# Where the last pair's scores stand against the first block inverse, and how the inversion's steps are dealt out

## The chip, the cores and the metric

One core of one Trainium2 chip runs the whole kernel as one program. The metric is device time in microseconds of that core, and the figure for a kernel is the median of its runs. Before the change it is 1244.08 us, the median of three runs from 1243.03 to 1244.97.

## The reference, cut to what matters

Four residual sub-layers over 512 positions of 1024 channels: a gated spatial mixer, a gated convolutional feed-forward layer, an RWKV-7 time mixer, and the feed-forward layer again, each behind an RMS norm. The change lies in the time mixer. With 16 heads of 64 channels it computes

```
...
r = xr @ w_r;  k = xk @ w_k;  v = xv @ w_v
...
def step(state, inp):                       # state (head, 64 values, 64 keys)
    sa = state @ a_t
    state = state * w_t + sa b_t^T + v_t k_t^T
    y_t = state @ r_t
...
y = group_norm(y) * ln_w + ln_b
bonus = sum(r * k * r_k) * v
return ((y + bonus) * (sigmoid(xg @ g1) @ g2)) @ w_o
```

Everything is in float32.

## The kernel before, in words

**Dense products.** A dense 128x512 product is made of three TensorE matmuls of high and low parts (lines 325, 326, 327). A group of 24 of them makes one block of 128 output channels. In the time mixer these groups are the *fill*: a generator that yields after every six matmuls (two blocks of 128 inputs), so that other work on TensorE can be put between the steps. `fill` is a chain of three generators: `projections` (keys and values), `gates` (the gate's first factor, lines 1135 and 1172 among others) and `project` (the output projection, `wo`). `gates` and `project` also yield when they have nothing to give: `gates` calls `idle` (line 1124: two matmuls whose result nobody uses) until the first group of heads has been normalised, and `project` yields nothing at all while the group's gated outputs are not yet emitted.

**The chunked scan.** The recurrence is done in 8 chunks of 64 positions, with heads in 8 pairs; pairs 0 to 3 are group 0, pairs 4 to 7 group 1. The stages, in the order of the program:

1. `pairs` makes, for each pair, decayed operands (lines 911 to 957, mostly VectorE), then the *scores* inside a chunk and the *turned keys* (`products`: matmuls at lines 973 and 988; VectorE's masked copies at line 977). A pair is three yields.
2. `invert(g)` inverts the triangular 64x64 matrices of group g: 25 yields. The first is taken before anything is woven. Then come 15 yields of substitution, on VectorE alone: lines 1069 and 1070, a product and an addition into the same tile, so that each waits for the one before it. Two transposes follow (line 1051), then eight yields of small TensorE products, 16 matmuls of 32x32 at a time (lines 1090 and 1093): the *block inverse's products*. ScalarE writes their results back into `ti[g]`.
3. `scan(g)`: for each chunk four small TensorE batches (lines 1301 and 1305, 1314, 1321, 1326) with copies by VectorE and ScalarE between them (1304, 1315 and 1316, 1325). The batch at line 1314 needs `ti[g]`. Behind every second chunk `finish` normalises the output (lines 1342 to 1366; the reciprocal root on GpSimd, line 389), and `gate` multiplies it with the gate (lines 1201 to 1214).

**What sets the order.** `weave(main, side, fill, rate, lag, side_rate)` runs `main`; after each of its yields it adds `rate` to a debt of fill steps and `side_rate` to a debt of side steps, and pays whole ones. `RATES` holds these numbers, one tuple for each of five weaves. Before the change the second weave (pairs 4 to 6 and the first yield of pair 7, with `invert(0)` at the side) and the weave for the last two yields of pair 7 both pay 2.2 steps of the inversion per yield of `pairs`. A layer below orders the recorded instructions on each engine's queue; each queue then runs strictly in that order.

**The values' bonus.** Inside a fill group of values, `value` puts two more matmuls between its steps: line 868, and line 883, whose result VectorE multiplies at line 885. Both, and the dense group itself, take a PSUM bank under the name `mm`, of which there are two. One is held by the dense group that is running, so the next dense group opens in the bank that line 885 has read.

Of the kernel before, what the change touches and what calls it, by code (L numbers as in the profile page):

```python
# [29 lines left out]
GN_EPS = 64e-5  # L30
C1 = -0.5 * math.exp(-0.5)

RATES = ((1.9, 2), (1.9, 6, 2.2), (0.66, 2, 1.15), (0.72, 2), (1.2, 6, 2.2))
LEAD = 1
WB = 4
FIRST0, WAIT, STEPS = 1, 1, (2, 2, 2, 2)
# [108 lines left out]
class Emit:  # L145
# [622 lines left out]
    def rwkv_main(self, r, ctx, gain):  # L768
# [226 lines left out]
        def pairs():  # L995

            units = [type("Unit", (), {})() for _ in range(KT)]

            def start(p):
                if p >= KT:  # L1000
                    return iter(())
                while p not in ks:
                    next(fill)
                if p == 0:
                    second_factors(p)
                return decay(p, units[p])

            yield from start(0)
            nxt = start(1)
            operands(0, units[0])  # L1010
            for _ in nxt:
                yield
            for p in range(KT):
                nxt = start(p + 2)
                if p + 1 < KT:
                    operands(p + 1, units[p + 1])
                parts = products(p, units[p])
                for n in range(3):
                    next(nxt, None)
                    with ExitStack() as behind:  # L1020
                        if n < 2:
                            behind.enter_context(tc.issue_after(self.last(mybir.EngineType.PE)))
                        next(parts, None)
                    yield
                done.add(p)

        def invert(g):

            tg = ti[g].rearrange("p i c t -> p (i c) t")
            Q = [(slice(64 * hd + 32 * b, 64 * hd + 32 * b + 32), slice(32 * b, 32 * b + 32))
                 for hd in range(2) for b in range(2)]

            def blocks(tag):
                return ip.tile([P, 32, 32], F32, tag=tag, bufs=1 if tag == "off" else 2, name=self.uid(tag))

            x = blocks("ix")
            pr = ip.tile([P, 272], F32, tag="pr", bufs=1, name=self.uid("pr"))
            cut = 24 * g  # L1040
            for us in (slice(0, cut), slice(cut, 32))[1 - g:]:
                for rows, cols in Q:
                    if us.start and g == 1:
                        V.tensor_copy(x[rows, us], tg[rows, us, cols])
                    else:
                        S.copy(x[rows, us], tg[rows, us, cols])
                if g == 1 and us.start == 0:
                    yield
            def turn(out, src):
                for bs in [slice(n, n + 8) for n in range(0, 32, 8)] if g == 1 else [slice(0, 32)]:  # L1050
                    V.transpose(out[:, bs], src[:, bs])

            tt = blocks("li")
            turn(tt.rearrange("p s t -> p t s"), x.rearrange("p u t -> p t u"))
            V.memset(tt.rearrange("p s t -> p (s t)")[:, 0:1024:33], 1.0)
            for _ in range(WAIT):
                yield
            for j in range(1, 31):
                ni = 31 - j
                to = tt[:, 0:j, j + 1:32]  # L1060
                if j == 1:
                    V.scalar_tensor_tensor(to[:, 0], tt[:, 1, 2:32], tt[:, 0, 1:2], to[:, 0], ALU.mult, ALU.add)
                elif ni == 1:
                    V.scalar_tensor_tensor(to[:, :, 0], tt[:, 0:j, j], tt[:, j, 31:32], to[:, :, 0], ALU.mult, ALU.add)
                else:
                    a = tt[:, j, j + 1:32].unsqueeze(1).to_broadcast([P, j, ni])
                    b = tt[:, 0:j, j].unsqueeze(2).to_broadcast([P, j, ni])
                    q = pr[:, 0:ni * j].rearrange("p (c i) -> p c i", i=ni)
                    V.tensor_tensor(q, a, b, ALU.mult)
                    V.tensor_tensor(to, to, q, ALU.add)  # L1070
                if j % 2 == 1:
                    yield

            z, y = blocks("ix"), blocks("li")
            turn(z.rearrange("p u t -> p t u"), tt)
            if g == 0:
                next(fill)
            turn(y.rearrange("p u t -> p t u"), tt.rearrange("p s t -> p t s"))
            yield
            off, own = blocks("off"), iter(Q)  # L1080
            for i in range(2):
                for hf in range(2):
                    ps = self.acc("aux" if g == 1 else "e").rearrange("p (u t) -> p u t", t=32)
                    us = slice(16 * hf, 16 * hf + 16)
                    for u in range(16):
                        for hd in range(2):
                            b0, b1 = Q[2 * hd][0], Q[2 * hd + 1][0]
                            n = 16 * hf + u
                            if i == 0:
                                nc.tensor.matmul(ps[b1, u, :], tg[b0, n, 32:64], z[b0, n, :], start=True, stop=True,  # L1090
                                                 tile_position=(b0.start, b1.start))
                            else:
                                nc.tensor.matmul(ps[b0, u, :], off[b1, n, :], y[b1, n, :], start=True, stop=True,
                                                 tile_position=(b1.start, b0.start))
                        if u % 8 == 7:
                            if i == 0:
                                rows, cols = next(own)
                                S.copy(tg[rows, :, cols], y[rows])
                            yield
                    for hd in range(2):  # L1100
                        b0, b1 = Q[2 * hd][0], Q[2 * hd + 1][0]
                        if i == 0:
                            S.copy(off[b1, us], ps[b1])
                        else:
                            S.copy(tg[b0, us, 32:64], ps[b0])

        gx, tail = [], []

        def gate_mix(k):
            with ExitStack() as behind:  # L1110
# [272 lines left out]
        def project():  # L1383

            for g in range(2):
                while g not in gated:
                    yield
                for m in range(2 - 2 * g, KT):
                    if m % 2 == 0:
                        w = wo.take()  # L1390
                    a = self.acc("mm")
                    yield from self.dense_steps(a, w, outs[g], c0=m % 2 * 512)
                    with ExitStack() as behind:
                        if left is None:
                            behind.enter_context(tc.issue_after(self.last(mybir.EngineType.DVE)))
                        V.tensor_tensor(self.h[m], self.h[m], a, ALU.add)
                    if g == 1:
                        self.absorb(m, gain)
# [13 lines left out]
        def until(gen, end):  # L1412
            for _ in gen:
                yield
                if end():
                    return


        fill = itertools.chain(projections(), gates(), project())
        gw, ga = {}, {}  # L1420
        main = pairs()
        self.weave(until(main, lambda: 3 in done), None, fill, *RATES[0], ktiles=STEPS[0])
        inv = invert(0)
        for _ in take(inv, FIRST0):
            pass
        self.weave(until(main, lambda: KT - 2 in done), inv, fill, *RATES[1], ktiles=STEPS[1])
        load(0, 0)
        ahead = invert(1)
        next(ahead)
        self.weave(main, inv, fill, *RATES[4], ktiles=STEPS[1])  # L1430
        for _ in inv:
            next(fill)
            self.step(ahead, (mybir.EngineType.PE,))
        ctx.close()
        ep = ctx.enter_context(tc.tile_pool(name="scan", bufs=1))
        inv = ahead
        r.sg = [ep.tile([P, T], F32R, name=f"sg{i}") for i in range(3)]
        for _ in range(LEAD):
            next(fill, None)
        self.weave(scan(0), inv, fill, *RATES[2], ktiles=STEPS[2])  # L1440
        for _ in inv:
            pass
        self.weave(scan(1, left.pop()), None, fill, *RATES[3], ktiles=STEPS[3])
        rest, left = left.pop(), None
# [80 lines left out]
```

## Time and profile before

| what | value |
|---|---|
| median of three runs | 1244.08 us |
| profiled execution, device time | 1245.55 us |
| profiled execution, span from first to last instruction | 1243.7 us |
| TensorE (PE) busy | 1226.8 us, 99% of the span |
| VectorE (DVE) busy | 851.1 us, 68% |
| ScalarE (ACT) busy | 633.1 us, 51% |
| GpSimd (POOL) busy | 81.4 us, 7% |
| mean granted TensorE clock | 0.996 |
| `pairs` 4 to 7 with the first inversion at the side | about 651 to 716 us of the span |
| first scan starts | 725.8 us |
| last dense step before the output projection of group 1 | ends about 848 us |

The profiled execution is one run of its own; the sums of the prediction are made on its scale. A TensorE row of the timeline gives a start and a modelled duration: dense 128x512 matmuls follow each other every 0.23 us although each is shown with 0.39, so the cost of one is read from start to start. The number in square brackets at the end of a row is the engine's idle time just ahead of it, with the instruction that released it.

### The profile page before, as it was taken

What the parts mean: (1) busy time and instruction counts of PE and PEld (TensorE: products, weight loads), DVE (VectorE), ACT (ScalarE), POOL (GpSimd) and SP (SyncE); (2) the same over time, 40 slices, a digit from 0 to 9 for tenths busy, and PEclk for the clock granted to TensorE, in tenths of its full rate; (3) what the DMA queues carried; (4) which work ended last, traced back from release to release, by engine and by line L of the source; (5) the groups of instructions that cost most, each with busy time, mean ns of one, the idle gap of its engine ahead of it and who ended that gap; (6) DMA issues with size and microseconds to landing.
All of it is one profiled execution on the core that took longest, in us unless ns stands there. A gap on an engine that the chain in (4) does not pass through costs nothing.

```text
span 1243.7 us, 19411 instructions
## 1 busy us (share of the span) xinstructions
PE 1226.8 (99%) x7535; PEld 1000.2 (80%) x7535; DVE 851.1 (68%) x1418; ACT 633.1 (51%) x1089; POOL 81.4 (7%) x106
## 2 busy tenths in 40 slices
PE   9999999999999999999999999999999999999997
PEld 6878888888888888877887777778888888888886
DVE  5566578888876454675899698776777777872323
ACT  6544455555554343466787667424544444543232
POOL 1100200000000001000000013222000000000000
PEclk9999999999999999999999899999999999999999
DMA  7232457887556776326888797654223223333332
GB/s 273 94 105 82 132 180 246 246 249 241 192 172 193 220 226 196 109 81 182 220 242 237 188 280 233 219 171 135 85 102 102 90 97 102 97 88 104 97 93 81
DMA packets 125133, 201.65 MB, mean 162 GB/s; under 512 B 39857, under 2 KB 63153, under 8 KB 125041
## 3 DMA queue, kind: packets, MB, share of 16 engines
q10 hardware_dynamic: 38976, 112.87, 29.5%
q1 hardware_dynamic: 86064, 87.54, 22.6%
q8 instruction: 59, 0.97, 0.3%
q14 instruction: 34, 0.27, 0.1%
HBM read 152.93 MB, written 47.45 MB: 161 GB/s over the span
## 4 chain that ended last, share of the span: by engine, by line
PE 91%; DVE 4%; DMA 3%; ACT 1%; issue 0%; SPq 0%; POOL 0%; DVEq 0%; POOLq 0%; ACTq 0%
PE mm L325 9%; PE mm L327 9%; PE mm L326 9%; PE aux L325 6%; PE aux L326 6%; PE aux L327 6%; PE e L325 6%; PE e L326 6%; PE us L325 6%; PE e L327 6%; PE us L327 6%; PE us L326 6%; PE us L1314 1%; PE aux L973 1%; PE aux L988 1%; PE us L1321 1%
## 5 line engine op out<-in xcount | busy, mean ns | idle before, releaser
L237 ACT CAST w<-w 128x512 fp32r<-128x512 f32 x340 | 206.5, 611 | 359.8 <-PE aux L327 92.6
L238 DVE TENSOR_TENSOR w<-w,w 128x512 fp32r<-128x512 f32 x340 | 230.5, 680 | 180.2 <-ACT w L237 179.6
L325 PE MATMUL mm<-mxh,w 128*128 128x512 f32 x408 | 167.9, 412 | 2.7 <-DVE rt L885 2.6
L327 PE MATMUL mm<-mxh,w 128*128 128x512 f32 x408 | 161.1, 395 | 0.0
L326 PE MATMUL mm<-mxl,w 128*128 128x512 f32 x408 | 160.6, 394 | 0.0
L325 PEld LDWEIGHTS mm<-mxh,w 128*128 128x128 f32 x408 | 77.0, 189 | 22.8 <-DVE rt L885 3.3
L327 PEld LDWEIGHTS mm<-mxh,w 128*128 128x128 f32 x408 | 77.0, 189 | 17.1 <-issue 0.8
L326 PEld LDWEIGHTS mm<-mxl,w 128*128 128x128 f32 x408 | 77.1, 189 | 16.2 <-issue 1.7
L575 ACT ACTIVATE cv<-z,par 128x512 f32<-128x512 f32 x88 | 71.7, 817 | 26.5 <-DVE z L573 21.2
L325 PE MATMUL aux<-mxh,w 128*128 128x512 f32 x216 | 84.5, 391 | 0.0
L325 PE MATMUL us<-mxh,w 128*128 128x512 f32 x216 | 84.5, 391 | 0.0
L327 PE MATMUL aux<-mxh,w 128*128 128x512 f32 x216 | 84.2, 390 | 0.0
L326 PE MATMUL aux<-mxl,w 128*128 128x512 f32 x216 | 84.1, 389 | 0.0
L326 PE MATMUL us<-mxl,w 128*128 128x512 f32 x216 | 84.1, 389 | 0.0
L327 PE MATMUL us<-mxh,w 128*128 128x512 f32 x216 | 84.1, 389 | 0.0
L354 POOL TENSOR_TENSOR ss<-ss,sq 128x512 f32<-128x512 f32 x24 | 31.7, 1323 | 761.1 <-ACT sq L352 761.1
L325 PE MATMUL e<-mxh,w 128*128 128x512 f32 x208 | 81.4, 391 | 0.0
L326 PE MATMUL e<-mxl,w 128*128 128x512 f32 x208 | 81.1, 390 | 0.0
L327 PE MATMUL e<-mxh,w 128*128 128x512 f32 x208 | 81.0, 389 | 0.0
L576 DVE SCALAR_TENSOR_TENSOR cv<-z,par,cv 128x512 f32<-128x512 f32 x88 | 66.0, 752 | 19.5 <-ACT cv L575 19.5
L577 DVE SCALAR_TENSOR_TENSOR cv<-z,par,cv 128x512 f32<-128x512 f32 x88 | 66.0, 752 | 2.9
L325 PEld LDWEIGHTS aux<-mxh,w 128*128 128x128 f32 x216 | 40.5, 188 | 9.0 <-issue 0.5
(1113 smaller groups left out, 2555.2 us busy)
## 6 DMA issues: line engine op xcount, KB each, us to landing
w<-in_wup ACTq DMA_DIRECT2D x88, 512.0 KB, 3.7
w<-in_wdn ACTq DMA_DIRECT2D x32, 512.0 KB, 3.7
st<-std SPq DMA_DIRECT2D x15, 640.0 KB, 6.6
w<-wkd ACTq DMA_DIRECT2D x16, 512.0 KB, 5.1
w<-wvd ACTq DMA_DIRECT2D x16, 512.0 KB, 5.1
w<-wod ACTq DMA_DIRECT2D x16, 512.0 KB, 4.2
w<-in_wdn ACTq DMA_DIRECT2D x16, 384.0 KB, 3.3
w<-in_wsu ACTq DMA_DIRECT2D x8, 512.0 KB, 3.7
```

The costliest lines, as they stand in the source:

```text
L237: nc.scalar.copy(hi[r, :n], src)
L238: (lo_eng or nc.vector).tensor_tensor(lo[r, :n], src, hi[r, :n].bitcast(F32), ALU.subtract)
L325: mm(acc, wh, xh, start=first, stop=False)
L326: mm(acc, wh, xl, start=False, stop=False)
L327: mm(acc, wl, xh, start=False, stop=last)
L354: nc.gpsimd.tensor_tensor(self.ss, self.ss, self.sq, ALU.add)
L575: nc.scalar.activation(c, z[:, 2:], AF.Identity, scale=cw(2, i), bias=self.p("conv_b", l * 44 + i))
L576: nc.vector.scalar_tensor_tensor(c, z[:, 1:T + 1], cw(1, i), c, ALU.mult, ALU.add)
L577: nc.vector.scalar_tensor_tensor(c, z[:, 0:T], cw(0, i), c, ALU.mult, ALU.add)
L973: nc.tensor.matmul(qs[hd][:, c - ch.start, :], bk[H[hd], c, C * hd:C * hd + P], ar[H[hd], c, :], start=True, stop=True)
L988: nc.tensor.matmul(qs[hd][:, c, :], bk[H[hd], c, C * hd:C * hd + P], dg[H[hd], c, :], start=True, stop=True)
L1314: nc.tensor.matmul((us, ux)[hd][H[hd], 1, i, :], ti[g][H[hd], i, c, :], wt[H[hd], i, :], start=True, stop=True)
```

## The change

```
-RATES = ((1.9, 2), (1.9, 6, 2.2), (0.66, 2, 1.15), (0.72, 2), (1.2, 6, 2.2))
+RATES = ((1.9, 2), (1.9, 6, 1.6), (0.66, 2, 1.15), (0.72, 2), (1.2, 6))
...
             turn(y.rearrange("p u t -> p t u"), tt.rearrange("p s t -> p t s"))
+            turned.append(g)
             yield
...
-        gx, tail = [], []
+        gx, tail, turned = [], [], []
...
-        self.weave(main, inv, fill, *RATES[4], ktiles=STEPS[1])
-        for _ in inv:
-            next(fill)
-            self.step(ahead, (mybir.EngineType.PE,))
+        self.weave(main, None, fill, *RATES[4], ktiles=STEPS[1])
+        for n, _ in enumerate(inv):
+            if turned and n % 2 == 0:
+                next(fill)
+            if turned:
+                self.step(ahead, (mybir.EngineType.PE,))
```

In the second weave the inversion of group 0 gets 1.6 steps per yield of `pairs` instead of 2.2. In the weave of the last pair it gets none. What is left of it comes behind the last pair, in a loop of its own. Once the transposes are recorded (`turned`), every second pass of that loop takes a fill step, and every pass takes a step of the inversion of group 1 (`ahead`). Before, the loop had one pass left; now it has ten, four of which take a fill step. Three lines are added, so line numbers past 1079 grow by one there: 1090 becomes 1091, 1301 becomes 1302, 1363 becomes 1364.

On TensorE, at the block inverse's first product, before. `mm` is a dense group or line 868's product, `e` the inverse's, `ti` the matrices, `ix` their transposed blocks:

```order
L325 MATMUL mm_6293<-mxh_5515,w_1020_6194 128x512
L326 MATMUL mm_6293<-mxl_5516,w_1020_6194 128x512
L327 MATMUL mm_6293<-mxh_5515,w_1020_6194 128x512
L868 MATMUL mm_6325<-cst,v_6291 128x128
L1090 MATMUL e_6306<-ix_6288,ti_4841 32x32 x16
L868 MATMUL mm_6325<-cst,v_6291 128x128 x3
L325 MATMUL mm_6293<-mxh_5522,w_1020_6194 128x512
```

The same place now, where the dense group of that name is called `mm_6277`, and line 868 is followed by the last pair's scores (`aux` and `us` from `ar` and `bk`):

```order
L325 MATMUL mm_6277<-mxh_5522,w_1020_6178 128x512
L868 MATMUL mm_6289<-cst,v_6275 128x128 x4
L326 MATMUL mm_6277<-mxl_5523,w_1020_6178 128x512
L327 MATMUL mm_6277<-mxh_5522,w_1020_6178 128x512
L325 MATMUL mm_6277<-mxh_5544,w_1020_6178 128x512
L326 MATMUL mm_6277<-mxl_5545,w_1020_6178 128x512
L327 MATMUL mm_6277<-mxh_5544,w_1020_6178 128x512
L973 MATMUL aux_6307<-ar_6137,bk_6143 128x128
L973 MATMUL us_6308<-ar_6137,bk_6143 128x128
```

The first product of the inverse moved from behind the first of line 868's matmuls to behind both halves of the last pair's scores, its turned keys and 36 more dense matmuls. From this place to the first batch of the scan TensorE now has 78 dense matmuls, and before 60.

On VectorE, the end of the substitution before, with line 885's product (`rt` from `mm` and `v`) and the transposes (`ix`, `li`):

```order
L1070 TENSOR_TENSOR li_5820<-li_5820,pr_5815 128x26x5
L1069 TENSOR_TENSOR pr_5815<-li_5820 128x108
L1070 TENSOR_TENSOR li_5820<-li_5820,pr_5815 128x27x4
L1069 TENSOR_TENSOR pr_5815<-li_5820 128x84
L1070 TENSOR_TENSOR li_5820<-li_5820,pr_5815 128x28x3
L885 TENSOR_TENSOR rt_4333<-mm_6277,v_6191 128x512
L1069 TENSOR_TENSOR pr_5815<-li_5820 128x58
L1070 TENSOR_TENSOR li_5820<-li_5820,pr_5815 128x29x2
L1064 SCALAR_TENSOR_TENSOR li_5820<-li_5820 128x30
L1051 STREAM_TRANSPOSE ix_6288<-li_5820 128x32x32
```

And now:

```order
L1070 TENSOR_TENSOR li_5820<-li_5820,pr_5815 128x26x5
L1069 TENSOR_TENSOR pr_5815<-li_5820 128x108
L885 TENSOR_TENSOR rt_4333<-mm_6261,v_6175 128x512
L1070 TENSOR_TENSOR li_5820<-li_5820,pr_5815 128x27x4
L1069 TENSOR_TENSOR pr_5815<-li_5820 128x84
L1070 TENSOR_TENSOR li_5820<-li_5820,pr_5815 128x28x3
L1069 TENSOR_TENSOR pr_5815<-li_5820 128x58
L1070 TENSOR_TENSOR li_5820<-li_5820,pr_5815 128x29x2
L1064 SCALAR_TENSOR_TENSOR li_5820<-li_5820 128x30
L1051 STREAM_TRANSPOSE ix_6447<-li_5820 128x32x32
```

Line 885's product moved ahead by three small steps of the substitution. What stands behind it up to the transposes, and the number of VectorE instructions up to there, is otherwise the same.

On TensorE, behind the last gate openings (`us` from `sg` and `gw`), before. Line 1363 transposes the last normalised output `y`:

```order
L1201 MATMUL us_8358<-sg_6631,gw_7954 128x256
L325 MATMUL mm_8389<-mxh_7795,w_1318_8215 128x512
L326 MATMUL mm_8389<-mxl_7796,w_1318_8215 128x512
L327 MATMUL mm_8389<-mxh_7795,w_1318_8215 128x512
L325 MATMUL mm_8389<-mxh_7805,w_1318_8215 128x512
L326 MATMUL mm_8389<-mxl_7806,w_1318_8215 128x512
L327 MATMUL mm_8389<-mxh_7805,w_1318_8215 128x512
L1363 MATMUL aux_8396<-cst,y_8185 128x128 x4
L325 MATMUL mm_8389<-mxh_7864,w_1318_8215 128x512
```

And now, where `mxh_8131` is the first gated output of group 1, made from those transposes:

```order
L326 MATMUL us_8374<-sg_6698,gwh_7890 128x256
L327 MATMUL us_8374<-sg_6697,gwl_7891 128x256
L1202 MATMUL us_8374<-sg_6699,gw_7886 128x256
L1364 MATMUL aux_8405<-cst,y_8205 128x128 x4
L325 MATMUL mm_8430<-mxh_8131,w_1328_8305 128x512
L325 MATMUL mm_8450<-mxh_8131,w_1329_8307 128x512
L326 MATMUL mm_8430<-mxl_8132,w_1328_8305 128x512
```

The two fill steps (12 dense matmuls of group 0's output projection) that stood around the transposes are no longer there; the 96 dense matmuls of group 1 follow at once. In between, at the end of the first scan, `idle` is called three times instead of two (six matmuls of line 1124 instead of four).

## The prediction

> **What bounds the kernel now.** I read the page first: busy times, slices, chain.
>
> ```profile
> span 1243.7 us, 19411 instructions
> PE 1226.8 (99%) x7535; PEld 1000.2 (80%) x7535; DVE 851.1 (68%) x1418; ACT 633.1 (51%) x1089; POOL 81.4 (7%) x106
> PEclk9999999999999999999999899999999999999999
> PE 91%; DVE 4%; DMA 3%; ACT 1%; issue 0%; SPq 0%; POOL 0%; DVEq 0%; POOLq 0%; ACTq 0%
> ```
>
> TensorE is the bound, so a change can win only where TensorE waits or is slow. The clock shows an 8 in one slice, near 700 us. The waits of TensorE name one large one, and the timeline has its places:
>
> ```profile
> PE mm L325 <- DVE rt L885: 2.6, 2, 2.3
> ...
> 684.11 0.50 PE L325 MATMUL mm<-mxh,w 128*128 128x512 f32 x1 [0.35 <-DVE rt L885]
> 694.31 0.40 PE L327 MATMUL mm<-mxh,w 128*128 128x512 f32 x1
> 696.99 0.50 PE L325 MATMUL mm<-mxh,w 128*128 128x512 f32 x1 [2.28 <-DVE rt L885]
> ```
>
> Twice a new dense group waits for its PSUM bank, which VectorE's line 885 must read first: 0.35 and 2.28 us. The second wait also costs clock. In stretches of 3.41 us set so that one boundary falls on the clock's drop:
>
> ```profile
> 694.55:697.97 3.42, 1.14 (x5) 0.85 (x5) 3.14 (x12) 1.84 (x4) 0.00 (x0) 1.00 0.92 239
> 697.97:701.38 3.41, 3.22 (x40) 2.60 (x40) 3.41 (x2) 0.92 (x2) 0.00 (x0) 0.50 0.47 154
> 701.38:704.79 3.41, 3.41 (x12) 2.83 (x12) 0.10 (x1) 3.20 (x6) 0.00 (x0) 0.50 0.00 0
> 704.79:708.21 3.42, 3.42 (x79) 2.77 (x78) 0.73 (x2) 1.40 (x3) 0.00 (x0) 1.00 0.79 197
> 1233.86:1237.27 3.41, 2.60 (x13) 1.34 (x12) 0.84 (x3) 0.81 (x2) 0.69 (x1) 1.00 0.48 161
> ```
>
> The columns are length, PE, PEld, DVE, ACT and POOL busy, then granted clock. After a stretch with PE busy 1.14 of 3.42 us, the clock is 0.50 for two stretches. After one with 2.60 (last row) it is not. What half a clock costs, from neighbouring starts:
>
> ```profile
> 703.01 0.63 PE L327 MATMUL mm<-mxh,w 128*128 128x512 f32 x1
> 703.44 0.63 PE L325 MATMUL mm<-mxh,w 128*128 128x512 f32 x1
> 705.69 0.39 PE L326 MATMUL mm<-mxl,w 128*128 128x512 f32 x1
> 705.92 0.39 PE L327 MATMUL mm<-mxh,w 128*128 128x512 f32 x1
> ```
>
> A dense matmul takes 0.43 us instead of 0.23, so 0.47 of the time is lost: 1.6 us in one stretch, 3.2 us in two. The Trainium skill's "TensorE: Matmul & The Clock Gate", section "Why this matters for your kernels", asks for no idle gaps over about 3 us; here 2.28 us were enough, so the measurement decides.
>
> **Part 1, the thinner dealing: does the wait for line 885 go?** Why line 885 is late is seen on VectorE, first in stretches of 20 us (DVE is the fourth figure), then row by row:
>
> ```profile
> 660.00:680.00 20.00, 19.44 (x179) 15.97 (x178) 19.86 (x46) 15.01 (x31) 0.11 (x1) 1.00 0.86 226
> 680.00:700.00 20.00, 17.18 (x126) 12.94 (x126) 19.27 (x46) 8.71 (x18) 0.61 (x2) 0.95 0.95 264
> ...
> 681.21 0.40 DVE L1069 TENSOR_TENSOR pr<-li 128x240 f32<-128x240 f32 x1
> 681.53 0.68 DVE L950 TENSOR_TENSOR kn<-kn,e 128x512 f32<-128x512 f32 x1
> 683.36 0.69 DVE L885 TENSOR_TENSOR rt<-mm,v 128x512 f32<-128x512 f32 x1
> 688.01 0.40 DVE L1070 TENSOR_TENSOR li<-li,pr 128x228 f32<-128x228 f32 x1
> 688.44 0.39 DVE L1069 TENSOR_TENSOR pr<-li 128x220 f32<-128x220 f32 x1
> 696.25 0.68 DVE L885 TENSOR_TENSOR rt<-mm,v 128x512 f32<-128x512 f32 x1
> 697.67 1.99 DVE L1051 STREAM_TRANSPOSE ix<-li 128x1024 f32<-128x1024 f32 x1
> 707.48 0.69 DVE L977 TENSOR_TENSOR lq<-aux,cst 128x512 f32<-128x512 f32 x1 [6.00 <-issue]
> ```
>
> VectorE is full (19.86 and 19.27 of 20 us) up to the transposes and idle only behind them (6.00 us). And the new order has the same number of instructions up to the transposes. A substitution step costs 0.32 us to the next start when something independent follows (681.21 to 681.53), and about 0.12 more when its own successor does (688.01 to 688.44: 0.43). I laid the new order on such intervals, 0.60 for a 128x512 operation; laid the same way, the old order meets its measured starts within 0.1 us.
>
> - First 885: a 128x512 product (`dg`, 0.60) comes in front of it for one step (0.32), and two more steps stand back to back (0.24). It starts 0.52 later, and the wait becomes 0.35 + 0.52 = 0.87.
> - Second 885: three small steps go behind it (0.75 by their intervals), but five more steps stand back to back (0.58). It starts only 0.2 sooner. TensorE comes 0.52 later, so the wait is 2.28 - 0.52 - 0.2 = 1.55.
>
> Together -0.2 us, and the 0.2 us that the first product waited for the transposes goes as well: -0.4 in all. The wait is split, not removed. Bounds: 0 (both as before) to -2.8 (both gone). I take -0.4, which is near the first since VectorE's work stays. The Trainium skill's "VectorE: DVE Perf Modes", section "The DRAIN you can't avoid", says that a semaphore between chained operations costs nothing extra; the rows show 0.12 for a successor. By that page the second wait would be 1.0 us and the sum 0.6 less.
>
> What follows: with 1.55 us idle, PE is busy 1.9 of 3.41 us, midway between the row that lost the clock (1.14) and the one that kept it (2.60). The latter holds small matmuls and modelled tails, 13 matmuls in all, so I think that the clock holds: -3.2 us. If not, 0.
>
> **Part 2, the last pair in front.** The same matmuls in another order, no new instruction. The last pair's masked copies (line 977) stand behind the transposes on VectorE in both orders. By the laid order the transposes begin 0.7 us later than the row's 697.67, so the copies end at about 703. TensorE needs the bank that they free at the turned keys. Between its wait at 696 (over at 696.8) and these stand 24 dense matmuls (5.5 us), both halves of the scores, and lines 868 and 883: the dense ones alone take it to 702.3. No wait: 0, at most +1. The 18 dense matmuls drawn forward need their weights sooner; each group still has its predecessor's 24 matmuls (5.5 us and more) to load behind: 0.
>
> **Part 3, the fill that is eaten.** Three more fill steps (18 dense matmuls, 4.1 us) are spent before the scan. They are missed later, in two places.
>
> ```profile
> 780.18 0.69 PE L1301 MATMUL us<-vu,st 128*64 128x64 f32 x16 [0.80 <-issue]
> 791.54 0.66 PE L1363 MATMUL aux<-cst,y 128*128 128x128 f32 x4 [0.46 <-DVE y L1357]
> 792.74 1.13 PE L1124 MATMUL e<-cst 128*128 128x256 f32 x4
> ```
>
> At the end of the first scan one step becomes a third `idle` call. The row shows one call, 1.1 us of TensorE for nothing: +1.1. Nothing dense stands there for two chunks, so copies between batches show; before, the waits there were 0.80 and 0.46. I take no difference, with bounds of -1.3 (those two gone) and +1.3 (as much again).
>
> The two other steps stood at the end of the second scan:
>
> ```profile
> 842.70 1.63 POOL L389 TENSOR_TENSOR gr<-rs,mhalf 128x8 f32<-128x8 f32 x1 [8.22 <-DVE rs L388]
> 844.58 0.69 DVE L1357 TENSOR_TENSOR y<-y,gr 128x512 f32<-128x512 f32 x1
> 844.81 0.28 PE L1201 MATMUL us<-sg,gw 96*128 96x256 f32 x1
> 844.93 0.40 PE L325 MATMUL mm<-mxh,w 128*128 128x512 f32 x1
> 846.35 0.60 PE L1363 MATMUL aux<-cst,y 128*128 128x128 f32 x4
> 846.98 0.61 DVE L1366 SCALAR_TENSOR_TENSOR rt<-aux,par,rt 128x128 f32<-128x128 f32 x2
> 847.51 0.47 DVE L1209 TENSOR_TENSOR rt<-rt,us 128x128 f32<-128x128 f32 x2
> 847.82 0.30 ACT L1213 CAST mxh<-rt 128x128 fp32r<-128x128 f32 x1 [1.42 <-DVE rt L1209]
> 848.17 0.49 PE L325 MATMUL mm<-mxh,w 128*128 128x512 f32 x1
> ```
>
> The openings end at 844.93. The 12 dense matmuls and the transposes fill TensorE to 848.17, just when the first gated output (847.82 + 0.30) is ready. Without them the transposes wait for `y` until 845.3 (844.58 + 0.69): 0.4. Then the chain over VectorE and ScalarE remains. VectorE's queue is unchanged up to line 1366 at 846.98, so the first dense matmul of group 1 still starts at about 848.1, and TensorE waits 845.7 to 848.1, another 2.4. Those 12 matmuls ran earlier, so all of it is lost: +2.7 (12 x 0.23). Bounds: +1.8 (if VectorE took line 1366 as soon as the transposes end, about 0.9 earlier) and +3.3. Idle by 2.8 of 3.2 us, TensorE is emptier here than where the clock fell: one stretch at half clock, +1.6, since nothing but dense work follows; two would be 3.2, none 0.
>
> **Part 4, the scan's start.**
>
> ```profile
> 728.28 0.68 PE L1314 MATMUL us<-wt,ti 64*64 64x64 f32 x16 [0.78 <-DVE wt L1304]
> ```
>
> Group 1's inversion starts earlier on VectorE, where the 6.00 us were idle. The first copy for the scan (line 1304) then stands behind 19 substitution steps instead of 11 and ends between 729 and 730 by the laid order. TensorE, 4.1 us of fill later and 3.6 us of waits and clock sooner, is there at 728.0 (728.28 - 0.78 + 4.1 - 3.6). A wait of 1 to 2 us replaces the 0.78: I take +0.5, with bounds of -0.8 (none left) and +2.
>
> **Sum, on the profiled execution's 1245.55 us:** -0.4 - 3.2 + 1.1 + 2.7 + 0.5 + 1.6 = +2.3, so 1247.85. That execution stands 1.47 us above the median of the runs. Half a clock in the middle is worth 3.2 us, and I cannot see how many of the timed runs lost it. The Trainium skill's "TensorE: Matmul & The Clock Gate", section "What's actually happening", calls the clock's window free-running: by it some runs would lose the clock and others not, which no trace here shows. I take off half of the difference, 0.7: **1247.1 us**, 0.24% above 1244.08. 0.2% of the median, 2.5 us, is about what a measurement can tell from no change, so slower starts at 1246.6 and faster ends at 1241.6.
>
> **The rivals.**
>
> - *The clock holds at the tail too* (0.3). For: the stretch boundaries may cut the idle time in two. Against: 2.28 us were enough at 697. Time: 1247.1 - 1.6 = 1245.5, no change that can be told. The 3 us rule of the Trainium skill's "TensorE: Matmul & The Clock Gate", quoted above, would make it this one.
> - *The middle wait still drops the clock* (0.2). For: 1.9 of 3.41 us busy is no nearer to 2.60 than to 1.14. The 3.2 us stay: 1247.1 + 3.2 = 1250.3, slower; with the tail's clock holding, 1248.7.
> - *Faster: VectorE's queue gets ahead of TensorE* (0.1). For: the thinner dealing leaves pair 7's operations closer together, and the queue's order is all that makes line 885 late; the laid times are mine, and no trace shows them. If the second 885 starts at 694.4, 1.6 us sooner than laid, TensorE waits at neither (-2.4 against the forecast), and VectorE stays ahead into the scan: 0.78, 0.80 and 0.46 go and the 0.5 is not paid (-2.5). With the clock holding at the tail: 1245.5 - 4.9 = 1240.6. Against: VectorE's 19.86 of 20 us, and an order that takes out only 0.75 us of steps.
> - My forecast (0.4) is 1247.1, its own range 1245 to 1249 from the bounds of parts 3 and 4.
>
> **How the numbers follow.** The forecast's range straddles 1246.6: I give 0.25 of its 0.4 to slower, 0.15 to no change. The first rival gives 0.24 to no change and 0.06 to slower, the second 0.2 to slower, the third 0.1 to faster. That is 0.1 faster, 0.39 no change, 0.51 slower. The range runs from 1243.0 (the third rival lies beyond it) to 1250.0 (beyond it the worse half of the second); about 2 in 10 lie outside.
>
> **What would show it.** In the changed trace: line 885 releasing TensorE after about 0.9 and 1.5 us near 684 and 696; a clock of 1.00 near 700; three idle calls near 790; a wait of about 0.4 us at line 1364 and of about 2.4 us at the first dense matmul behind it, and half a clock after that. It would be wrong if both waits for line 885 are gone, or if the tail's wait is under 1 us.

## The result, and the profile after

| what | before | after |
|---|---|---|
| median | 1244.53 us (4 runs, 1243.03 to 1245.04) | 1253.98 us (4 runs, 1252.67 to 1254.80) |
| profiled execution, device time | 1245.55 us | 1253.96 us |
| span | 1243.7 us | 1252.2 us |
| mean granted clock in the runs | 0.996 (the profiled one) | 0.996, 0.997, 0.994, 0.996 |

The changed kernel takes 1.0077 times as long, with a 95% interval of 1.0060 to 1.0094: 9.5 us slower. The forecast was 1247.1, 3.0 us above the median known then, and its range ended at 1250.0. The page of the changed kernel begins like this:

```profile
span 1252.2 us, 19428 instructions
PE 1229.0 (98%) x7539; PEld 1000.6 (80%) x7539; DVE 852.4 (68%) x1418; ACT 632.8 (51%) x1089; POOL 82.7 (7%) x106
```

TensorE is busy for 2.2 us more and the span is 8.5 us longer, so most of the loss is time in which TensorE waits. Its waits, with the total, the number and the longest:

```profile
PE mm L325 <- ACT mxh L1214: 2.1, 1, 2.1
PE mm L325 <- DVE h L1194: 1.7, 1, 1.7
PE mm L325 <- DVE rt L885: 1.6, 1, 1.6
...
PE mm L1136 <- ACT mxh L237: 1.3, 1, 1.3
PE e L923 <- ACT sq L913: 1.2, 2, 0.7
...
PE us L1315 <- DVE wt L1305: 1.1, 2, 0.8
...
PE mm L868 <- ACT v L854: 0.8, 1, 0.8
```

Of the rows shown, the first is the wait that was forecast for the tail. The third is what is left of the two waits for line 885. The second and the fourth, for an addition to `h` and for a gate mix, were in no part of the prediction. Their places, from the timeline of TensorE:

```profile
671.56 1.16 PE L923 MATMUL e<-cst,sq 128*128 128x128 f32 x8 [0.57 <-ACT sq L913]
...
697.49 0.50 PE L325 MATMUL mm<-mxh,w 128*128 128x512 f32 x1 [1.59 <-DVE rt L885]
...
733.16 0.68 PE L1315 MATMUL us<-wt,ti 64*64 64x64 f32 x16 [0.84 <-DVE wt L1305]
...
756.82 0.57 PE L1136 MATMUL mm<-mxh,w 128*128 128x512 f32 x1 [1.31 <-ACT mxh L237]
...
815.05 0.74 PE L325 MATMUL mm<-mxh,w 128*128 128x512 f32 x1 [1.68 <-DVE h L1194]
...
854.42 0.63 PE L1364 MATMUL aux<-cst,y 128*128 128x128 f32 x4 [0.32 <-DVE y L1358]
857.18 0.72 PE L325 MATMUL mm<-mxh,w 128*128 128x512 f32 x2 [2.12 <-ACT mxh L1214]
```

The granted clock (the first figure behind the five engines' busy times), in stretches of 3.41 us on the grid that the drops at 757.10 and 815.13 set (17 stretches apart):

```profile
695.67:699.09 3.42, 1.83 (x8) 1.24 (x7) 3.11 (x12) 3.33 (x6) 0.00 (x0) 1.00 0.77 207
...
753.69:757.10 3.41, 2.10 (x65) 1.75 (x65) 1.90 (x4) 3.28 (x7) 0.44 (x1) 1.00 0.89 252
757.10:760.51 3.41, 3.38 (x16) 1.50 (x17) 1.84 (x3) 3.27 (x6) 0.00 (x0) 0.50 0.28 99
...
811.71:815.13 3.42, 1.74 (x21) 1.15 (x19) 3.33 (x5) 0.00 (x0) 1.22 (x2) 1.00 0.82 279
815.13:818.54 3.41, 3.41 (x24) 2.54 (x25) 1.40 (x4) 0.37 (x1) 0.00 (x0) 0.50 0.86 265
...
852.68:856.09 3.41, 2.06 (x16) 1.64 (x15) 2.90 (x11) 1.00 (x4) 0.67 (x1) 1.00 0.46 154
856.09:859.50 3.41, 2.32 (x10) 1.94 (x11) 2.81 (x12) 1.09 (x4) 0.00 (x0) 1.00 0.00 0
```

The clock holds near 700 and at the tail. It falls for one stretch each behind the two waits that the prediction had not listed, at 757 and at 815. At the tail the boundary at 856.09 cuts the idle time in two, and with 2.06 and 2.32 us busy in the two stretches the clock holds.

### The profile page after: what moved, and what is told of

The parts are those of the page before. It is cut to its first block, busy times and chain, and to the rows that moved or that the text cites. A ratio compares the mean times of both kernels' runs of the same rounds, so it can differ in the third digit from the quotient of the medians.

```text
span 1252.2 us, 19428 instructions
## 1 busy us (share of the span) xinstructions
PE 1229.0 (98%) x7539; PEld 1000.6 (80%) x7539; DVE 852.4 (68%) x1418; ACT 632.8 (51%) x1089; POOL 82.7 (7%) x106
## 4 chain that ended last, share of the span: by engine, by line
PE 91%; DVE 4%; DMA 2%; ACT 2%; issue 1%; POOL 0%; SPq 0%; DVEq 0%; POOLq 0%; ACTq 0%
PE mm L325 9%; PE mm L327 9%; PE mm L326 9%; PE aux L325 6%; PE aux L327 6%; PE aux L326 6%; PE e L325 6%; PE e L326 6%; PE us L325 6%; PE e L327 6%; PE us L327 6%; PE us L326 6%; DMA w<-in_wsv 1%; PE aux L973 1%; PE us L1315 1%; DVE li L1070 1%
```

## What the new waits are

**At 815: the additions that end the gate's generator.** VectorE around it, in the changed kernel:

```profile
811.42 1.09 DVE L1358 TENSOR_TENSOR y<-y,gr 128x512 f32<-128x512 f32 x1 [1.04 <-POOL gr L389]
812.55 1.00 DVE L258 TENSOR_TENSOR gw<-w,gw 32x512 fp32r<-32x512 f32 x1
813.58 0.69 DVE L238 TENSOR_TENSOR gwl<-w,gwh 128x512 fp32r<-128x512 f32 x1
814.30 0.69 DVE L1194 TENSOR_TENSOR h<-h,mm 128x512 f32<-128x512 f32 x1
```

The next dense group needs the bank that line 1194 reads. That addition stands behind the normalisation of `y`, which waits 1.04 us for GpSimd, and behind two operations that split group 1's gate weights. In the kernel before, the normalisation is over long before the addition, and TensorE waits for neither:

```profile
803.95 1.09 DVE L1357 TENSOR_TENSOR y<-y,gr 128x512 f32<-128x512 f32 x1 [1.04 <-POOL gr L389]
...
813.39 0.69 DVE L1193 TENSOR_TENSOR h<-h,mm 128x512 f32<-128x512 f32 x1
```

It is the same normalisation in both, the fifth of the eight: before, it ends 8 us ahead of the addition, and now 2 us. The fill has been moved forward against the scan, and so its last addition has come up to it.

**At 757: the gate's mixes on ScalarE.** ScalarE in the changed kernel ahead of that wait:

```profile
747.81 1.05 ACT L1099 COPY ti<-li 32x1024 f32<-32x1024 f32 x1 [1.17 <-DVE li L1051]
...
750.51 2.10 ACT L1099 COPY ti<-li 32x1024 f32<-32x1024 f32 x2
752.51 1.49 ACT L873 COPY vt<-aux 64x256 f32<-64x256 f32 x4
754.03 0.72 ACT L1115 ACTIVATE sq<-h,par 128x512 f32<-128x512 f32 x1
754.78 0.75 ACT L1330 COPY y<-e 64x256 f32<-64x256 f32 x2
755.55 0.58 ACT L1104 COPY off<-aux 32x512 f32<-32x512 f32 x1
756.15 0.62 ACT L237 CAST mxh<-sq 128x512 fp32r<-128x512 f32 x1
```

ScalarE works without a pause and is late with the mix (lines 1115 and 237). What fills it are the copies of group 1's block inverse (lines 1099 and 1104). Group 1's products stood on TensorE at 761 to 778 us before the change and stand at 748 to 768 now; the loop steps group 1's inversion nine times instead of once.

## The experiments

The kernel before was run beside each of them, with medians of 1244.5 to 1245.0; each ratio below is against those runs. Theory A: the fill that is spent in the loop is missed later, and at more places than the two that I had counted. Theory B: it is group 1's earlier inversion that costs the time. Diffs are against the kernel that is named.

### The fill alone

Kernel before:

```
-LEAD = 1
+LEAD = 4
```

> The kernel before with one number changed: four fill steps instead of one stand directly in front of the first scan. As many dense matmuls (18, 4.1 us) are drawn forward as by the change, nothing else moves. Theory A (the fill that is spent early is missed later: at the end of the gate's factors 3.5 us with a clock drop, in a third idle call 0.9, at the tail 2.8): about 7 us over the kernel before, less the 0.8 us wait at the scan's start, so 1250 to 1251.5. Theory B (the loss in the scans comes from group 1's inversion, which the change starts nine steps earlier): only tail and idle call show, 3.7 - 0.8, so about 1247.5. If drawing fill forward costs nothing: 1244.5.

Measured: 1252.31 us, ratio 1.0067 (1.0052 to 1.0082), 7.7 us slower. A holds, 0.8 us above its range: three fill steps drawn forward cost nearly what the whole change costs, with nothing else moved. Its waits contain the tail's and the addition's:

```profile
PE mm L325 <- ACT mxh L1213: 2.1, 1, 2.1
PE mm L325 <- DVE h L1193: 1.7, 1, 1.7
```

and at its tail the idle time falls into one stretch, so that there the clock does drop:

```profile
850.47:853.92 3.45, 1.01 (x6) 0.72 (x6) 3.45 (x15) 0.99 (x4) 0.00 (x0) 1.00 0.38 135
853.92:857.34 3.42, 3.42 (x10) 2.63 (x8) 1.40 (x6) 0.59 (x2) 0.20 (x4) 0.50 0.00 0
```

The wait is 2.12 us in both kernels, and here it costs one stretch at half clock on top (1.6 us by the prediction's price), because nearly all of it falls into one stretch.

### One step forward, one step back

Kernel before, `LEAD = 2` and `LEAD = 0`.

> The kernel before with two fill steps in front of the first scan instead of one: one step (6 dense matmuls, 1.4 us) is drawn forward. If the price of fill goes by the step (7.7 us for three in the run with three drawn forward), 1247.2. If only the tail's half is missed (1.4 us, no third idle call, and the gate's last additions still find the second gate's weights behind them): 1246.0. Nothing missed: 1244.6.

Measured: 1246.76 us, ratio 1.0018 (1.0009 to 1.0026), 2.2 us slower. It lies between the two cases; its tail waits 1.3 us (line 1213) and it has no third idle call and no wait for the addition. One step costs 2.2 us and three cost 7.7. Three times the first would be 6.6, which the two intervals do not tell from 7.7, so it stays open whether the price goes by the step.

> The kernel before with no fill step in front of the first scan: one step is kept back. Theory (fill is worth more late than early, but the kernel before has just enough of it at the end): nothing is gained late, since TensorE does not wait at the tail, and the first batch of the scan loses its cover: the wait for line 1304 grows from 0.8 to 2.2 us, about 1246. Rival (each step kept back saves what a step drawn forward costs): 1242.

Measured: 1250.19 us, ratio 1.0052 (1.0039 to 1.0064), 5.7 us slower: both cases missed. Nothing is gained late, as the theory said, but keeping a step back costs far more than 1.4 us, and not where the theory had it: the longest wait for line 1304 is 1.0 us, and not 2.2. In its trace

```profile
PE mm L325 <- issue: 1.9, 1, 1.9
```

stands at 852, among the dense matmuls behind the tail. The profile names no cause. The wait ends 0.1 us behind an addition to `h` on VectorE (line 1396, from 851.64, 0.68 us), which reads a bank of the name `mm`; that fits, but it is timing alone. The rest of the 5.7 us is not assigned; it stays open. In these runs a fill step moved either way in front of the scan is lost time.

### The order without the loop's two bills

Kernel before: the thinner dealing, and the rest of the inversion dealt out within the last pair, so that the loop has one pass and one fill step as before.

```
-RATES = ((1.9, 2), (1.9, 6, 2.2), (0.66, 2, 1.15), (0.72, 2), (1.2, 6, 2.2))
+RATES = ((1.9, 2), (1.9, 6, 1.6), (0.66, 2, 1.15), (0.72, 2), (1.2, 6, 4.7))
```

> The kernel before with two numbers changed: 1.6 steps of the inversion per yield of pairs 4 to 6 as in the change, and 4.7 in place of 2.2 in the last pair's weave, so that the loop behind it still has one pass and one fill step. Nearly the changed order up to the block inverse (the last pair's scores and turned keys stand in front of it), with the fill and group 1's inversion as before. Theories A and B alike: the 4.3 us that the changed kernel gains between 690 and 712 us (waits and clock) stay, 2.8 to 4 are lost again at the inverse's products, which have fewer dense matmuls between them, and nothing is missed later: 1243 to 1244.5. Rival: the gain in the middle is an accident of the profiled executions (the clock falls in some of the runs only): 1246 to 1248.5.

Measured: 1244.74 us, ratio 1.0004 (0.9992 to 1.0016): no change. All of the inverse's products stand behind the last pair's scores and turned keys here, as in the changed kernel, with dense matmuls still dealt out between them, and it costs nothing. So neither the thinner dealing nor the place of the last pair makes the kernel slower by itself; the loop does. It does not win either, though it has one wait for line 885 instead of two:

```profile
PE mm L325 <- DVE rt L885: 1.6, 1, 1.6
...
PE e L923 <- ACT sq L913: 1.2, 2, 0.7
```

### Taking the loop's bills away, one at a time

Changed kernel. One fill step in the loop:

```
-            if turned and n % 2 == 0:
+            if turned and n == 2:
```

> The changed kernel, but the loop behind the last pair takes one fill step and not four; group 1's inversion is still stepped nine times in it. Theory A: the 7.2 us of the gate's end, the idle call and the tail come back, and 1 to 3 us are lost at the inverse's products, which stand with less between them: 1248 to 1250. Theory B: only tail and idle call come back (3.7), and the loss at the inverse eats 1 to 3 of that: 1251.5 to 1253.5.

Measured: 1249.92 us, ratio 1.0043 (1.0027 to 1.0059). The tail's wait for line 1214 and the one for the addition are gone, and 4.1 us come back, as A had it. In its trace the clock falls behind the block inverse's products instead, from 724.8 us for two stretches, and once more at 796.5.

One step of group 1's inversion in the loop:

```
-            if turned:
+            if n == 8:
                 self.step(ahead, (mybir.EngineType.PE,))
```

> The changed kernel, but group 1's inversion is stepped once in the loop (in its last pass), as before the change, and not nine times; four fill steps as in the change. Theory A: the fill decides, 1254 within 0.7. Theory B: the 1.7 us lost between 733 and 790 us (with the clock drop at 757) and the 3.5 at 800 to 816 go: about 1249; if only the collision at 757 goes, 1252.3.

Measured: 1251.77 us, ratio 1.0063 (1.0042 to 1.0085), with runs from 1249.3 to 1258.2. By its median 2.2 us come back, between the two theories, and the interval overlaps that of the changed kernel. The loop's ten passes count from 0, so the step stands in the last but one. The edit takes back only a part of what it was meant to. TensorE's products of group 1 stand late again in its trace (from 764.3 us), but VectorE is through with the transposes at the same time as in the changed kernel (the last starts at 747.1 in both), and ScalarE's copies of line 1099 still stand at 748 to 759. So the mix still waits 0.9 us, now without a loss of clock, and the 2.2 us are not the price of the earlier inversion. The trace is that of the slowest of the six runs. A new wait stands in it at 781, inside a batch of which 15 of 16 matmuls have run, and the clock falls there for two stretches, from 781.3 to 788.1. What it is for, and whether the faster runs have it, the profile does not show:

```profile
PE us L1322 <- issue: 2.7, 1, 2.7
```

Both edits together:

> The changed kernel, whose loop takes one fill step and one step of group 1's inversion, as before the change: the last pair in front and the thinner dealing are left, with the inverse's products in a row. If the two bills add up (4.1 for the fill in front of the scan, 2.2 for the early inversion, by the runs that take away one of them), 1247.7. If the order alone costs nothing, as where 4.7 steps per yield were dealt out in the last pair: 1244.7.

Measured: 1248.80 us, ratio 1.0027 (1.0015 to 1.0039). The interval holds the 1247.7 of the two bills and not the 1244.7 of an order that costs nothing: fill and inversion together are 5.2 us of the 9.5. The other 3.9 are a third one, larger than the 1 to 3 us that I had allowed for it: the inverse's products stand in a row in this loop with hardly anything dense between them, and each batch waits for what the last one gives.

```profile
PE e L1094 <- issue: 1.2, 1, 1.2
...
PE e L1094 <- ACT off L1104: 0.9, 1, 0.9
```

The clock falls behind them, for two stretches, of which the first is shown:

```profile
721.74:725.15 3.41, 2.12 (x109) 1.91 (x111) 3.10 (x8) 2.38 (x5) 0.00 (x0) 1.00 1.01 275
725.15:728.57 3.42, 3.42 (x64) 2.74 (x56) 1.81 (x5) 1.15 (x2) 0.00 (x0) 0.50 1.07 378
```

That is what the three fill steps are for. In the changed kernel they cover these products, so that of the 7.7 us a net bill of 3.0 to 4.1 is left (1251.77 - 1248.80 and 1253.98 - 1249.92).

### Repairs on the changed kernel

0.62 fill steps per yield of the second scan, instead of 0.72:

> The changed kernel with 0.62 fill steps per yield of the second scan instead of 0.72: the third idle call goes and one fill step of group 0's output projection stands again in front of the last transposes. Theory (the fill is missed only where nothing else covers a chain, and the chunks of the second scan have cover to spare): idle call 0.9 and half of the tail 1.4 come back, 1251.7. Rival (each step that is kept back is missed in the chunks): 1254.

Measured: 1251.70 us, ratio 1.0059 (1.0046 to 1.0072), 2.3 us less than the changed kernel. The number is the forecast one, but only half of its working is. One fill step stands again ahead of the last transposes, and the tail's wait is down from 2.12 us, as forecast. The third idle call (794.27 in the changed kernel) is gone too, but its time does not come back: TensorE waits as long for `y` at that place, where the changed kernel does not wait. What else makes up the 2.3 us is not assigned.

```profile
794.66 0.66 PE L1364 MATMUL aux<-cst,y 128*128 128x128 f32 x4 [1.11 <-DVE y L1358]
...
854.80 0.49 PE L325 MATMUL mm<-mxh,w 128*128 128x512 f32 x1 [1.23 <-ACT mxh L1214]
```

The additions to `h` ahead of the gate weights' split:

```
-            gw[1] = gate_weights(ga["w"])
             for m in range(2):
...
                 V.tensor_tensor(self.h[m], self.h[m], accs[m], ALU.add)
+                if m == 1:
+                    gw[1] = gate_weights(ga["w"])
                 yield
```

> The changed kernel, but the split of group 1's gate weights (lines 258 and 238 on VectorE) is written behind the two additions to h that end the gate's generator, and not ahead of them: the first of these additions then stands directly behind the normalisation of y. Theory (the 1.68 us that TensorE waits for it at 815 are the price of VectorE's order there): the wait goes, and with it the chance of the clock drop behind it (1.6): 1251 to 1252.3. Rival (VectorE is late at this place anyway, by its wait for GpSimd's root): no change, 1254.

Measured: 1251.21 us, ratio 1.0053 (1.0041 to 1.0065), 2.8 us less. The addition starts directly behind the normalisation, 1.8 us sooner, and TensorE waits for it no more:

```profile
811.33 1.09 DVE L1359 TENSOR_TENSOR y<-y,gr 128x512 f32<-128x512 f32 x1 [1.04 <-POOL gr L389]
812.46 0.69 DVE L1193 TENSOR_TENSOR h<-h,mm 128x512 f32<-128x512 f32 x1
```

The wait of 1.68 us and what follows from it are shown to be VectorE's order at this place, which the drawn-forward fill had made to matter.

Both repairs:

> The changed kernel with both repairs that were tried alone: 0.62 fill steps per yield of the second scan (alone 1251.7), and the additions to h ahead of the split of the gate weights (alone 1251.2). If they stand for different terms, 1254.0 - 2.3 - 2.8 = 1248.9; if they are the same idle time told twice, about 1251.

Measured: 1250.55 us, ratio 1.0042 (1.0030 to 1.0054). That is nearer to 1251 than to 1248.9: they do not add up. The tail waits as with the first repair alone (1.2 us for line 1215), and the wait for the addition is gone as with the second; what of the time the two share, the runs do not tell.

The copies of the block inverse off ScalarE:

```
-                                S.copy(tg[rows, :, cols], y[rows])
+                                (V.tensor_copy if g == 1 else S.copy)(tg[rows, :, cols], y[rows])
```

> The changed kernel, but the four copies of group 1's block inverse into its matrices (line 1099, about 1.05 us each on ScalarE) run on VectorE. Theory (they stand on ScalarE ahead of the gate's mixes, whose cast at line 237 then comes 1.31 us late, and the clock falls behind that wait in some runs): 1254.0 - 1.3 to 1254.0 - 2.9, so 1251 to 1252.7, with the wait for line 237 under 0.4. Rival (VectorE pays instead: the scan's own copies at lines 1305 and 1316 come late): 1253.5 to 1256.

Measured: 1253.49 us, ratio 1.0070 (1.0056 to 1.0084). The wait for line 237 is gone and the mix is ready 1.1 us sooner:

```profile
755.07 0.62 ACT L237 CAST mxh<-sq 128x512 fp32r<-128x512 f32 x1
```

So the cause of the wait is shown. Its price is not: the median moved by 0.5 us, where 1.3 to 2.9 were forecast. That lies at the edge of the rival's range, but the rival's sign is missing: the waits for VectorE's copy (line 1305) are 1.1 us in all, as in the changed kernel. In its profiled execution the clock no longer falls at 757. It still falls at 814 and falls, as in the run with the fill alone, at 855.

### Where the middle's gain lies

Kernel before, with other rates for the inversion, all with one pass and one fill step in the loop: 1.9 and then 3.4; 2.05 and then 2.9.

> The kernel before with 1.9 steps of the inversion per yield of pairs 4 to 6 (between 2.2 and 1.6) and 3.4 in the last pair's weave, so that the loop has one pass and one fill step as before. Theory (the thinner dealing trades a shorter wait for line 885 against a second wait for ScalarE's squares at line 923, 0.57 us, and against block inverse products that stand closer together, 1.65): a middle rate pays part of each, 1244 to 1245. Rival (the two costs set in only below 1.9): 1242.5 to 1243.5.

Measured: 1242.96 us, ratio 0.9992 (0.9981 to 1.0003). The median is 2.0 us lower, but the interval includes no change. One wait for line 885, and a second for the squares, as with 1.6:

```profile
PE mm L325 <- DVE rt L885: 1.6, 1, 1.6
PE e L923 <- ACT sq L913: 1.2, 2, 0.7
```

> The kernel before with 2.05 steps of the inversion per yield of pairs 4 to 6 and 2.9 in the last pair's weave; loop of one pass and one fill step as before. Theory (each wait is set by where single instructions land in the two queues, not by how full VectorE is): the second wait at line 923 is gone or there as a whole (0 or 0.57), and the wait for line 885 is one of 1.6 or two as before; time between the 1243.0 of the run with 1.9 and 1244.9. Rival (the waits go smoothly with the rate): half-way waits, 0.3 at line 923 and 2 us for line 885.

Measured: 1245.59 us, ratio 1.0002 (0.9994 to 1.0011). The time is 0.7 us above the theory's range. Two waits for line 885 and one for the squares:

```profile
PE mm L325 <- DVE rt L885: 2.5, 2, 2.1
...
PE e L923 <- ACT sq L913: 0.7, 1, 0.7
```

The waits come and go as a whole. That each is set by where single instructions land in a queue fits this; with two rates it is not more than a fit.

Kernel before, line 883's product in a bank of the other name:

```
-            q = bank()
+            q = self.acc("aux")
             nc.tensor.matmul(q, wb, rt[g][:, i, :], start=True, stop=True)
```

> The kernel before, with the product of line 883 always in a bank of the name aux, not in mm; the dense group then need not wait for VectorE's line 885. Theory (the wait is one for a bank): the 2.6 us at 684 and 697 go and with them the clock drop where a run had it: 1241 to 1242. Rival (VectorE is full there, and TensorE waits for it at the next place, the last pair's scores, which use aux): 1244 to 1245.

Measured: 1245.03 us, ratio 0.9996 (0.9988 to 1.0005): no change, as the rival had it, though at another place than it said. The dense group waits for line 885 no more, and line 868 waits for ScalarE's copy of `v` instead:

```profile
PE mm L868 <- ACT v L854: 1.7, 1, 1.7
```

## Why the prediction was wrong

The direction was right and the size was not. The sum was made against the profiled execution, and the two profiled executions can be laid side by side. The waits are read from the traces; a stretch at half clock is put at 1.6 us, the prediction's price:

| step of the prediction | forecast | trace |
|---|---|---|
| waits of pairs 5 to 7 | -0.4 | +0.1 |
| clock near 700 | -3.2 | -3.2 |
| third idle call | +1.1 | +1.1 |
| tail, two waits | +2.7 | +2.4 |
| tail, clock | +1.6 | 0 |
| scan's start | +0.5 | +0.1 |
| addition at 815, wait and clock | not seen (0) | +3.3 |
| mix at 757, wait and clock | not seen (0) | +2.7 |
| sum | +2.3 | +6.5 of 8.4 |

- **Part 1, waits.** The second wait for line 885 was forecast at 1.55 us and is 1.59. The first was to grow to 0.87 and is gone: TensorE came later, behind a second wait for the squares (0.57 at 671.56) that I had not looked for. Line 868's wait of 0.79 for ScalarE is new too. Together 1.59 + 0.57 + 0.79 against 2.28 + 0.35 and the 0.2 of the first product makes +0.1.
- **Part 1, clock.** The clock held with TensorE busy 1.83 of 3.42 us, as forecast. But on the median this was hardly worth 3.2 us. In 75 further runs of the kernel before, 38 had a mean clock of 0.998 or 0.999 and a median of 1244.1 us; 34 had 0.996 or 0.997 and a median of 1245.4; three were lower still. A stretch of 3.41 us at half clock takes 0.0014 off the mean. The drop at the very end, which every kept trace has, takes 0.0012 in the trace of before (3.0 us of it lie inside the span). By these figures half of the runs lost no stretch near 700. The prediction took off 0.7 us because it could not see this; it is one likely reason why the measured 9.5 us lie above the trace's 8.4.
- **Part 2** held as far as the last pair goes. The run with the same fill shows that order at no cost. That the inverse's products would cost time when nothing dense is left between them (3.9 us in the run with both edits) is in no part of the prediction; in the changed kernel the loop's fill covers them.
- **Part 3 is the step that failed.** "They are missed later, in two places" was the error. The tail's waits (2.44 us for 2.7) and the third idle call (twelve records of `idle` in the trace now, and before eight, two for each matmul) came as forecast. The waits around the idle calls, for which the prediction took no difference, came to the same sum (between 780 and 797 us, 0.80 and 0.46 us before, 0.29 and 0.99 now). But the rest of the second scan had no term at all. I asked which waits exist and would change, and not which work had been hidden by the fill and would come to light. The addition to `h` was such a work; its wait of 1.68 us and the clock behind it are in no row of the trace of before. The run with the fill alone has that wait, and the run with the additions first loses it. The amount that was moved was too small as well: the three steps carry, besides the 18 dense matmuls, eight records of line 868 and two of line 883 to the front of the scan, which at 0.11 and 0.25 us from start to start is about 1.4 us more than the 4.1.
- **Part 3, tail's clock.** Forecast to fall, held here by the boundary that cuts the idle time in two, and fell in the run with the fill alone. That was my first rival's mechanism, with a chance of 0.3.
- **Part 4** priced the earlier inversion on one VectorE copy only: 0.84 us there instead of 0.78. That this is near the forecast +0.5 is luck. TensorE was to be there at 728.0 and came at 732.3, and the copy was to end by 730 and ended at 733.1. What the moved steps bring along was not counted, so it stood in the sum at nothing: ScalarE's copies (lines 1099 and 1104) collide with the gate's mixes. The wait at 757 is shown to come from them, and its price in the median is open between 0.5 us and 2.7.
- Of the other 1.9 us of the trace's difference, 0.65 is no part of the change. Group 1's first scores, where both orders are still the same, start that much later:

```profile
648.93 0.27 PE L973 MATMUL aux<-ar,bk 64*128 64x128 f32 x1
```

```profile
649.58 0.27 PE L973 MATMUL aux<-ar,bk 64*128 64x128 f32 x1
```

The first is the kernel before, the second the changed one. About 1.2 us is not assigned.

Of the signs that the prediction named, all but two came true (the first wait for line 885 and the half clock behind the tail), and neither of its signs of being wrong appeared. The signs watched the places that it had thought of.

No kernel of these runs beats the one before by more than the measurement can tell; the run with a rate of 1.9 comes nearest.

## What to carry to other kernels

Filler work that is moved forward does not vanish from one place but from every place behind: go through all that it had covered, and ask of each engine's queue there what would be late if TensorE came earlier, not only which waits the trace already shows. A step of another generator that is moved brings all its instructions along, the copies on a quiet engine too. And a gain in granted clock that one profiled execution promises is worth its share of the runs only, so read the mean clock of several runs first.

## What the runs showed of the hardware

- Whether an idle time costs the clock depends on where the 3.41 us stretch begins. The tail's wait of 2.12 us cost nothing in the changed kernel (stretches with 2.06 and 2.32 us busy) and one stretch at half clock with the fill alone (1.01 us busy). The Trainium skill's "TensorE: Matmul & The Clock Gate", section "What's actually happening", calls the window free-running; the traces agree: the drops of one trace lie on one grid (757.10 and 815.13 in the changed kernel, 17 stretches apart), which stands elsewhere in each run.
- The busy time alone does not decide, and these runs give no threshold. Stretches with 1.83 of 3.42 us busy (changed kernel, at 696) and with 1.54 of 3.41 (additions first, at 852) kept the clock. One with 1.61 (line 883 in another bank, at 695) lost it, and at the wait for the addition 1.74 kept it with the fill alone and lost it in the changed kernel. Stretches with 2.10 us busy (65 matmuls, all but one of them 32 or 64 wide) and 2.12 (109) lost it. That small matmuls count for less would explain the last two; no run tested it.
